# The two halves of a split weight chunk queued three blocks apart

## The chip, the cores and the metric

The kernel runs on one core of a Trainium2 chip. The metric is the time of one execution on the device in microseconds; lower is better. The time of before is the median of three runs.

## What is computed

The reference is a model of two parts on 512 tokens of width 1024, all in float32. The first part has a SwiGLU feed-forward, a mixer (sparse attention with 8 heads beside an S5 state-space branch), a second SwiGLU and a gated projection. The second part has two layers, each with an RG-LRU branch and an mLSTM branch, and a last RMS norm:

```python
h = x
h = h + 0.5 * swiglu(rmsnorm(h, norm_ffn1), w1, w3, w2)
z = rmsnorm(h, norm_mix) @ w_in
h = h + concat([nsa_attention(...), s5_mixer(...)]) @ w_out
h = h + 0.5 * swiglu(rmsnorm(h, norm_ffn2), ...)
h = h + sigmoid(rmsnorm(h, norm_ple) @ w_ple_gate) * (p @ w_ple)
x = rmsnorm(h, norm_final)
for l in range(2):
    u = (rms_norm(x, g) * (1 + scale) + shift) @ w_in[l]
    rg_x, rg_z, ml_x, ml_o, ml_z = split(u)
    y_rg = rglru(conv(rg_x), ...) * silu(rg_z)
    y_ml = mlstm_branch(conv(ml_x), ml_o, ...) * silu(ml_z)
    x = x + gate * (concat([y_rg, y_ml]) @ w_out[l])
return rms_norm(x, final_g)
```

Almost all of the work is products of the activations with weights that are read once.

## The kernel before

The 512 tokens lie along the free dimension, so that every product is a 128x128 block of weights against a 128x512 tile of activations, summed in PSUM. To keep float32 accuracy each operand is split in a high and a low part, and every block takes three matmuls (`mm3`, lines 121 to 127): high weight by high activation (L125), high weight by low activation (L126), low weight by high activation (L127).

The weights come as a stream of 304 chunks of eight blocks, packed on the host in the order in which the program asks for blocks (class `Stream`, lines 56 to 118). A chunk passes three steps. SyncE loads it (`wstage`, three buffers); ScalarE copies it, rounded, into the high part (`whi`, L96, four buffers); VectorE subtracts the high part from the loaded chunk and so gives the low part (`wlo`, L98, four buffers). TensorE then uses the two parts, eight blocks one after the other. Chunks 0 and 1 are split in halves, and GpSimd makes the second low half of chunk 1.

All of this is laid out by one program in one order, and each engine carries out its own instructions in the order in which the program put them into its queue. So what counts is where in the program an instruction is put. `get` (L109) is called once for each block, ahead of the block's matmuls, and it also puts the later chunks' steps into the queues: with the call for block 4 of chunk c, ScalarE's high part and VectorE's low part of chunk c + 2 and SyncE's load of chunk c + 4 (L114). While `hold` is set, at the end of a stage, only what is needed is put, and `release` (L71) makes up for it.

Between the calls of `get` the program puts the other steps: in the SwiGLU stages (L263) the gates on VectorE and ScalarE, and in the two layers a list written out by hand (`LAYER`, L1384), whose entries are short: `P10` is the product with column block 10 of the input weights, `U10` the use of its result, `rg1`, `rq1`, `rs2` the gates, the square root and the scan of the RG-LRU (L1839, L1863, L1868), `hn1`, `f1`, `F1` steps of the mLSTM head (L1743 to L1789), `rz2` its gate by silu. The output product of a layer follows the list; its result is added to the residual at L1938.

The names of tiles: `wstage`, `whi`, `wlo` as above; `xnh`, `xnl` the parts of the normalized activations; `pahead`, `pbhead`, `pagates`, `paout` and the like PSUM tiles of the two alternating banks, named by the stage; `rth`, `ra`, `rt`, `ry` of the RG-LRU; `n`, `dn`, `hr` of the mLSTM head's norm; `ymh`, `yml`, `yrh`, `yrl` high and low parts of the output product's right side; `t` of the SwiGLU gate; `s5yg`, `s5gw`, `cA`, `cAh` of the mixer.

Of the kernel before, what the change touches and what calls it, by code (L numbers as in the profile page):

```python
# [21 lines left out]
F32 = mybir.dt.float32  # L22
F32R = mybir.dt.float32r
I32 = mybir.dt.int32
BF = mybir.dt.bfloat16
AF = mybir.ActivationFunctionType
# [9 lines left out]
CH = 8  # L36
# [14 lines left out]
def room(pool, name):  # L51
    if GAPS[name]:
        pool.tile([128, GAPS[name] // 4], F32, name="gap", bufs=1)


class Stream:
# [2 lines left out]

    AHEAD = 2  # L60
    SPLIT = 2

    def __init__(self, k, dram, nchunks):
        self.k, self.dram, self.n = k, dram, nchunks
        self.order = []
        self.stage, self.hi, self.lo = {}, {}, {}
        self.loaded = self.split_done = 0
        self.pos = 0
        self.hold = False

    def release(self):  # L71

        self.hold = False
        self.split(self.pos // CH + 1 + self.SPLIT)

    def load(self, upto):
        k = self.k
        while self.loaded < min(upto, self.n):
# [3 lines left out]
            self.stage[c] = t  # L82
            self.loaded += 1

    def split(self, upto):
        k = self.k
        while self.split_done < min(upto, self.n):
            c = self.split_done
            self.load(c + 1)
            st = self.stage.pop(c)  # L90
            hi = k.whi.tile([128, CH * 128], F32R, name="whi")
            lo = k.wlo.tile([128, CH * 128], F32R, name="wlo")
            n = 2 if c < 2 else 1
            for i in range(n):
                s = slice(i * CH * 128 // n, (i + 1) * CH * 128 // n)
                k.nc.scalar.activation(hi[:, s], st[:, s], AF.Copy)  # L96
                eng = k.nc.gpsimd if c * i == 1 else k.nc.vector
                eng.tensor_sub(lo[:, s], st[:, s], hi[:, s].bitcast(F32))  # L98
            self.hi[c], self.lo[c] = hi, lo
            self.split_done += 1  # L100
            self.load(c + 1 + self.AHEAD)

    def align(self, n):
# [5 lines left out]
    def get(self, *blocks):  # L109

        n = len(blocks)
        c, r = divmod(self.pos, CH)
        assert r + n <= CH
        self.split(c + 1 + (0 if self.hold else self.SPLIT if r >= CH // 2 else self.SPLIT - 1))  # L114
        self.order += list(blocks)
        self.pos += n
        s = slice(r * 128, (r + n) * 128)
        return self.hi[c][:, s], self.lo[c][:, s]
# [1842 lines left out]
def body(tc, ins, out, dbg):  # L1961
    nc = tc.nc
    with ExitStack() as ctx:
# [6 lines left out]
        room(k.wst, "base")  # L1970
        k.whi = pool("whi", Stream.SPLIT + 2)
        k.wlo = pool("wlo", Stream.SPLIT + 2)
        k.work = pool("work", 2)
# [251 lines left out]
```

## Time and profile before

| | before |
|---|---|
| median of three runs | 1997.06 us |
| lowest and highest | 1995.61 and 1997.36 us |
| the profiled execution | 1996.86 us |
| its span | 1995.1 us |
| mean granted TensorE clock | 0.982 |
| TensorE busy | 1931.2 us |
| VectorE busy | 1311.4 us |
| ScalarE busy | 821.4 us |

The span runs from the first to the last instruction; the execution's own time is 1.8 us longer. The granted clock is a share of the full 2.4 GHz; where it was not 1 it was 0.5, that is 1.2 GHz. A timeline row gives the start of an instruction, its length and, in brackets, how long its engine had idled ahead of it and what ended that. The ends of matmuls are modelled, so that for TensorE the starts are what is read.

### The profile page before, as it was taken

To read this page: it belongs to the slowest core of one execution; us is meant where nothing else is said; L and a number is where in the kernel's file an instruction comes from. 1 tells how busy PE (TensorE), PEld (TensorE's weight loads), DVE (VectorE), ACT (ScalarE), POOL (GpSimd) and SP (SyncE) were. 2 spreads that over 40 slices of the span, in tenths; PEclk is the share of its full clock that TensorE was granted. 3 is DMA by queue.
4 is the path that set the end of the run, shared out by engine and by line. 5 is a ranking of instruction groups with operands and counts; after the bars stand their busy time and mean duration, and the time that the engine had idled before them with its cause. 6 is when DMAs were issued, how large, how long until landed. Compare 5 with 4: busy or idle time off the path is not lost. (4 is left out here: it accounts for less than half of the span.)

```text
span 1995.1 us, 24709 instructions
## 1 busy us (share of the span) xinstructions
PE 1931.2 (97%) x9320; PEld 1581.3 (79%) x9320; DVE 1311.4 (66%) x2157; ACT 821.4 (41%) x1233; POOL 164.4 (8%) x225
## 2 busy tenths in 40 slices
PE   8999999998999999999999799999999899999997
PEld 6888888887867888888878687888888677887886
DVE  7766576678655575665666675887763666877843
ACT  5323232436555432232244445555432354555521
POOL 1000000111233100000001100101000100101001
PEclk9999999998899999999999899999999899999999
DMA  5335445465301365455433143222242243222241
GB/s 184 103 116 154 158 139 159 143 194 171 103 1 33 117 218 180 158 197 190 162 104 92 55 147 118 74 75 86 88 153 87 64 156 109 70 89 86 74 155 56
DMA packets 101400, 240.10 MB, mean 120 GB/s; under 512 B 24472, under 2 KB 37528, under 8 KB 101280
## 3 DMA queue, kind: packets, MB, share of 16 engines
q1 hardware_dynamic: 100592, 237.82, 37.6%
q8 instruction: 73, 1.20, 0.2%
q10 hardware_dynamic: 688, 0.70, 0.1%
q14 instruction: 47, 0.39, 0.1%
HBM read 216.19 MB, written 21.10 MB: 119 GB/s over the span
## 5 line engine op out<-in xcount | busy, mean ns | idle before, releaser
L98 DVE TENSOR_TENSOR wlo<-wstage,whi 128x1024 fp32r<-128x1024 f32 (+1 forms) x305 | 377.3, 1245 | 147.6 <-ACT whi L96 143.8
L96 ACT ACTIVATE whi<-wstage 128x1024 fp32r<-128x1024 f32 (+1 forms) x306 | 314.0, 1045 | 139.9 <-PE pasecond L126 43.1
L276 ACT ACTIVATE t<-t 128x512 f32<-128x512 f32 x44 | 27.9, 634 | 158.5 <-DVE t L275 158.5
L127 PE MATMUL pahead<-xnh,wlo 128*128 128x512 f32 x208 | 81.3, 391 | 3.4 <-DVE wlo L98 3.4
L125 PE MATMUL pahead<-xnh,whi 128*128 128x512 f32 x208 | 83.3, 400 | 0.0
L153 POOL TENSOR_TENSOR nacc<-nacc,nsq 128x512 f32<-128x512 f32 x20 | 26.8, 1343 | 680.9 <-ACT nsq L149 680.9
L126 PE MATMUL pahead<-xnl,whi 128*128 128x512 f32 x208 | 81.1, 390 | 0.0
L125 PE MATMUL pbfirst<-xnh,whi 128*128 128x512 f32 x176 | 70.4, 400 | 7.6 <-ACT whi L96 6.5
L125 PE MATMUL pbhead<-xnh,whi 128*128 128x512 f32 x192 | 76.9, 400 | 0.0
L1509 DVE SCALAR_TENSOR_TENSOR conv<-cpad,vec,conv 128x512 f32<-128x512 f32 x96 | 72.2, 752 | 5.6
L127 PE MATMUL pbhead<-xnh,wlo 128*128 128x512 f32 x192 | 75.5, 393 | 0.0
L126 PE MATMUL pbhead<-xnl,whi 128*128 128x512 f32 x192 | 75.3, 392 | 0.0
L126 PE MATMUL pbfirst<-xnl,whi 128*128 128x512 f32 x176 | 69.5, 395 | 0.3 <-DVE xnl L222 0.3
L127 PE MATMUL pbfirst<-xnh,wlo 128*128 128x512 f32 x176 | 69.2, 393 | 0.0
L125 PE MATMUL pbsecond<-xnh,whi 128*128 128x512 f32 x176 | 68.9, 392 | 0.0
L125 PE MATMUL pafirst<-xnh,whi 128*128 128x512 f32 x176 | 68.7, 390 | 0.0
L127 PE MATMUL pafirst<-xnh,wlo 128*128 128x512 f32 x176 | 68.6, 390 | 0.0
L127 PE MATMUL pbsecond<-xnh,wlo 128*128 128x512 f32 x176 | 68.5, 389 | 0.0
L126 PE MATMUL pbsecond<-xnl,whi 128*128 128x512 f32 x176 | 68.5, 389 | 0.0
L126 PE MATMUL pafirst<-xnl,whi 128*128 128x512 f32 x176 | 68.5, 389 | 0.0
L127 PE MATMUL pasecond<-xnh,wlo 128*128 128x512 f32 x176 | 68.5, 389 | 0.0
L125 PE MATMUL pasecond<-xnh,whi 128*128 128x512 f32 x176 | 68.5, 389 | 0.0
(762 smaller groups left out, 5229.9 us busy)
## 6 DMA issues: line engine op xcount, KB each, us to landing
wstage<-in_wpack_dram SPq DMA_DIRECT2D x304, 512.0 KB, 3.7
adaw<-in_wada_dram SPq DMA_DIRECT2D x48, 512.0 KB, 4.5
scr_v<-vv SPq DMA_DIRECT2D x16, 256.0 KB, 2.2
vr<-scr_v SPq DMA_DIRECT2D x16, 256.0 KB, 4.4
xr<-scr_x SPq DMA_DIRECT2D x16, 256.0 KB, 5.8
h<-in_xT_dram SPq DMA_DIRECT2D x8, 256.0 KB, 5.8
s5vw<-scr_wq SPq DMA_DIRECT2D x64, 32.0 KB, 2.0
s5vb<-in_s5bq_dram SPq DMA_DIRECT2D x8, 256.0 KB, 2.7
```

The lines of the kernel that those rows point to most:

```text
L96: k.nc.scalar.activation(hi[:, s], st[:, s], AF.Copy)
L98: eng.tensor_sub(lo[:, s], st[:, s], hi[:, s].bitcast(F32))
L125: mm(ps, w[0], x[0], start=start, stop=False)
L126: mm(ps, w[0], x[1], start=False, stop=False)
L127: mm(ps, w[1], x[0], start=False, stop=stop)
L153: k.nc.gpsimd.tensor_add(self.acc[1], self.acc[1], sq)
L276: nc.scalar.activation(t1, t1, AF.Silu)
L1509: v.scalar_tensor_tensor(c, xp[:, 1 + j:1 + j + T], w(j), c, op0=OP.mult, op1=OP.add)
```

## The change

The step that put both parts of a chunk into the queues is taken apart. The high part of chunk c + 2 is now put into ScalarE's queue with the call for block 3 of chunk c, one block earlier than before. The low part is put into VectorE's queue, and the load of chunk c + 4 into SyncE's, with the call for block 6, two blocks later. The two parts, which were put together, are three blocks apart. `hold` and `release` work as before, and the first two chunks too.

```diff
@@ -60,4 +60,5 @@
     AHEAD = 2
     SPLIT = 2
+    HI, LO = 3, 6
 
     def __init__(self, k, dram, nchunks):
@@ -65,5 +66,5 @@
         self.order = []
         self.stage, self.hi, self.lo = {}, {}, {}
-        self.loaded = self.split_done = 0
+        self.loaded = self.high_done = self.low_done = 0
         self.pos = 0
         self.hold = False
@@ -83,20 +84,37 @@
             self.loaded += 1
 
-    def split(self, upto):
+    def pieces(self, c):
+        n = 2 if c < 2 else 1
+        return [slice(i * CH * 128 // n, (i + 1) * CH * 128 // n) for i in range(n)]
+
+    def high(self, upto):
+
         k = self.k
-        while self.split_done < min(upto, self.n):
-            c = self.split_done
+        while self.high_done < min(upto, self.n):
+            c = self.high_done
             self.load(c + 1)
-            st = self.stage.pop(c)
-            hi = k.whi.tile([128, CH * 128], F32R, name="whi")
-            lo = k.wlo.tile([128, CH * 128], F32R, name="wlo")
-            n = 2 if c < 2 else 1
-            for i in range(n):
-                s = slice(i * CH * 128 // n, (i + 1) * CH * 128 // n)
-                k.nc.scalar.activation(hi[:, s], st[:, s], AF.Copy)
-                eng = k.nc.gpsimd if c * i == 1 else k.nc.vector
-                eng.tensor_sub(lo[:, s], st[:, s], hi[:, s].bitcast(F32))
-            self.hi[c], self.lo[c] = hi, lo
-            self.split_done += 1
+            self.hi[c] = k.whi.tile([128, CH * 128], F32R, name="whi")
+            for s in self.pieces(c):
+                k.nc.scalar.activation(self.hi[c][:, s], self.stage[c][:, s], AF.Copy)
+                if c < 2:
+                    self.low_piece(c, s)
+            self.high_done += 1
+
+    def low_piece(self, c, s):
+        k = self.k
+        if c not in self.lo:
+            self.lo[c] = k.wlo.tile([128, CH * 128], F32R, name="wlo")
+        eng = k.nc.gpsimd if c == 1 and s.start else k.nc.vector
+        eng.tensor_sub(self.lo[c][:, s], self.stage[c][:, s], self.hi[c][:, s].bitcast(F32))
+
+    def split(self, upto):
+
+        self.high(upto)
+        while self.low_done < min(upto, self.n):
+            c = self.low_done
+            if c > 1:
+                self.low_piece(c, self.pieces(c)[0])
+            del self.stage[c]
+            self.low_done += 1
             self.load(c + 1 + self.AHEAD)
 
@@ -112,5 +130,7 @@
         c, r = divmod(self.pos, CH)
         assert r + n <= CH
-        self.split(c + 1 + (0 if self.hold else self.SPLIT if r >= CH // 2 else self.SPLIT - 1))
+        if not self.hold:
+            self.high(c + self.SPLIT + (r >= self.HI))
+        self.split(c + 1 + (0 if self.hold else self.SPLIT - 1 + (r >= self.LO)))
         self.order += list(blocks)
         self.pos += n
```

In the changed file the lines behind the class stand 20 lower, and the subtraction is L108. Two places show what moves on VectorE.

The first is in layer 0, between the gates of the RG-LRU (`rg1`) and product `P10`. Before, the low part of chunk 204 stood ahead of the steps `rq1`, `hn1` and `rs2`; `rth`, `ra` and `rt` are tiles of the RG-LRU, `n` is the mLSTM head's:

```order
L1805 TENSOR_TENSOR yml<-n_10426,ymh 128x512
L98 TENSOR_TENSOR wlo<-wstage,whi 128x1024
L1854 TENSOR_TENSOR rth<-rth,conv 128x512
L1855 TENSOR_SCALAR ra<-ra 128x512
L1857 SCALAR_TENSOR_TENSOR rt<-rth,ra 128x512
L1858 SCALAR_TENSOR_TENSOR ra<-rt,ra 128x512
L1854 TENSOR_TENSOR rth<-rth,conv 128x512
L1855 TENSOR_SCALAR ra<-ra 128x512
L1857 SCALAR_TENSOR_TENSOR rt<-rth,ra 128x512
L1858 SCALAR_TENSOR_TENSOR ra<-rt,ra 128x512
L1760 SCALAR_TENSOR_TENSOR n_10790<-sig,pahead_10779 128x512
L1760 SCALAR_TENSOR_TENSOR n_10805<-sig,pbhead_10794 128x512
```

Now the same rows go by, and the low part of chunk 204 stands behind the last row of the scan (`ry`); the wlo behind `rz` is that of chunk 205:

```order
L1875 TENSOR_SCALAR ra<-ra 128x512
L1877 SCALAR_TENSOR_TENSOR rt<-rth,ra 128x512
L1878 SCALAR_TENSOR_TENSOR ra<-rt,ra 128x512
L1780 SCALAR_TENSOR_TENSOR n_10786<-sig,pahead_10775 128x512
L1780 SCALAR_TENSOR_TENSOR n_10801<-sig,pbhead_10790 128x512
L1890 SCALAR_TENSOR_TENSOR rth<-rth 128x512
L1891 TENSOR_TENSOR rth<-rth,ra 128x512
L1892 TENSOR_SCALAR ra<-ra 128x512
L1894 SCALAR_TENSOR_TENSOR ry<-ra,rth 128x512
L108 TENSOR_TENSOR wlo<-wstage,whi 128x1024
L1539 SCALAR_TENSOR_TENSOR rz<-rz,pahead_10811 128x512
L108 TENSOR_TENSOR wlo<-wstage,whi 128x1024
```

The first low part of the rows of before moved past 14 rows, to the place where the next low part had stood. Layer 1 has the same.

The second is at the start of the output product of layer 0 (`yrl`, `yml` are low parts of its right side). Before, the first low part here is that of chunk 224 and the last that of chunk 225:

```order
L1882 TENSOR_TENSOR ry<-ry,rz 128x512
L1805 TENSOR_TENSOR yrl<-ry,yrh 128x512
L98 TENSOR_TENSOR wlo<-wstage,whi 128x1024
L1795 TENSOR_TENSOR n_11736<-n_11736,pc 128x512
L1795 TENSOR_TENSOR n_11751<-n_11751,pc 128x512
L1882 TENSOR_TENSOR ry<-ry,rz 128x512
L1519 SCALAR_TENSOR_TENSOR zs<-zs,pahead_11881 128x512
L1813 SCALAR_TENSOR_TENSOR n_11736<-n_11736,hg_5926,zs 128x512
L1805 TENSOR_TENSOR yrl<-ry,yrh 128x512
L1805 TENSOR_TENSOR yml<-n_11736,ymh 128x512
L98 TENSOR_TENSOR wlo<-wstage,whi 128x1024
```

Now the first is that of chunk 223 and the last that of chunk 224:

```order
L1902 TENSOR_TENSOR ry<-ry,rz 128x512
L108 TENSOR_TENSOR wlo<-wstage,whi 128x1024
L1825 TENSOR_TENSOR yrl<-ry,yrh 128x512
L1815 TENSOR_TENSOR n_11732<-n_11732,pc 128x512
L1815 TENSOR_TENSOR n_11747<-n_11747,pc 128x512
L1902 TENSOR_TENSOR ry<-ry,rz 128x512
L1539 SCALAR_TENSOR_TENSOR zs<-zs,pahead_11877 128x512
L1833 SCALAR_TENSOR_TENSOR n_11732<-n_11732,hg_5922,zs 128x512
L1825 TENSOR_TENSOR yrl<-ry,yrh 128x512
L1825 TENSOR_TENSOR yml<-n_11732,ymh 128x512
L108 TENSOR_TENSOR wlo<-wstage,whi 128x1024
```

The low part of chunk 224 moved past seven rows, and that of chunk 223 came down to a place just ahead of the first `yrl`.

## Rows read from the trace of the kernel before

**Rows 1.** The page, part 1: busy time, share of the span, instructions.

```profile
PE 1931.2 (97%) x9320; PEld 1581.3 (79%) x9320; DVE 1311.4 (66%) x2157; ACT 821.4 (41%) x1233; POOL 164.4 (8%) x225
```

**Rows 2.** The page, part 5: the low parts: busy, mean ns, idle before.

```profile
L98 DVE TENSOR_TENSOR wlo<-wstage,whi 128x1024 fp32r<-128x1024 f32 (+1 forms) x305 | 377.3, 1245 | 147.6 <-ACT whi L96 143.8
```

**Rows 3.** TensorE's waits: line waited for, us in all, times, longest.

```profile
PE pm L195 <- DVE ncol L213: 5.8, 3, 2.5
...
PE pahead L127 <- DVE wlo L98: 3.4, 2, 1.7
...
PE pc L1793 <- DVE hr L1786: 1.7, 2, 0.9
```

**Rows 4.** Timeline of VectorE, layer 0: start, length, instruction, idle before it.

```profile
1322.07 1.23 DVE L98 TENSOR_TENSOR wlo<-wstage,whi 128x1024 fp32r<-128x1024 f32 x1 [2.83 <-ACT whi L96]
...
1325.27 0.43 DVE L1855 TENSOR_SCALAR ra<-ra 128x512 f32<-128x512 f32 x1 [1.37 <-ACT ra L1849]
...
1333.95 1.23 DVE L1874 TENSOR_TENSOR_SCAN ry<-ra,rth 128x512 f32<-128x512 f32 x1
1335.09 1.20 DVE L98 TENSOR_TENSOR wlo<-wstage,whi 128x1024 fp32r<-128x1024 f32 x1
```

**Rows 5.** Timeline of TensorE there.

```profile
1328.57 0.39 PE L127 MATMUL pbhead<-xnh,wlo 128*128 128x512 f32 x1
...
1329.93 0.39 PE L127 MATMUL pbhead<-xnh,wlo 128*128 128x512 f32 x1
```

**Rows 6.** Timeline of VectorE, the same place of layer 1.

```profile
1762.69 1.20 DVE L98 TENSOR_TENSOR wlo<-wstage,whi 128x1024 fp32r<-128x1024 f32 x1
```

**Rows 7.** Timeline of TensorE there.

```profile
1756.57 0.39 PE L127 MATMUL pbhead<-xnh,wlo 128*128 128x512 f32 x1
```

**Rows 8.** Timeline of VectorE, around the output product of layer 0.

```profile
1448.61 1.22 DVE L1874 TENSOR_TENSOR_SCAN ry<-ra,rth 128x512 f32<-128x512 f32 x1
...
1470.39 0.69 DVE L1805 TENSOR_TENSOR yml<-n,ymh 128x512 fp32r<-128x512 f32 x1
```

**Rows 9.** Timeline of TensorE there.

```profile
1448.69 0.39 PE L127 MATMUL pbhead<-xnh,wlo 128*128 128x512 f32 x1
...
1460.62 0.65 PE L1793 MATMUL pc<-ident,hr 128*128 128x128 f32 x4 [0.86 <-DVE hr L1786]
...
1468.41 0.39 PE L127 MATMUL paout<-yrh,wlo 128*128 128x512 f32 x1
```

**Rows 10.** Timeline of VectorE, the convolutions of layer 0.

```profile
1172.83 0.69 DVE L1546 TENSOR_TENSOR xcl<-xcs,xch 128x512 fp32r<-128x512 f32 x1
```

**Rows 11.** Timeline of TensorE there.

```profile
1174.23 0.39 PE L127 MATMUL pagates<-xnh,wlo 128*128 128x512 f32 x1
```

**Rows 12.** Timeline of VectorE at the first gate.

```profile
35.06 1.23 DVE L98 TENSOR_TENSOR wlo<-wstage,whi 128x1024 fp32r<-128x1024 f32 x1
```

**Rows 13.** Timeline of TensorE at the first gate and in the mixer.

```profile
36.95 0.50 PE L125 MATMUL pbfirst<-xnh,whi 128*128 128x512 f32 x1 [0.84 <-DVE t L275]
...
485.66 0.50 PE L125 MATMUL pamix<-xnh,whi 128*128 128x512 f32 x1 [1.47 <-ACT whi L96]
```

**Rows 14.** The page, part 6: loads, KB each, us to landing.

```profile
wstage<-in_wpack_dram SPq DMA_DIRECT2D x304, 512.0 KB, 3.7
```

**Rows 15.** Timeline of TensorE at two waits of before.

```profile
463.97 0.76 PE L125 MATMUL pbmix<-xnh,whi 128*128 128x512 f32 x1 [4.83 <-DVE ropeo L612]
...
1393.19 0.50 PE L127 MATMUL pahead<-xnh,wlo 128*128 128x512 f32 x1 [1.72 <-DVE wlo L98]
```

**Rows 16.** Windows of TensorE: us, busy (instructions), granted clock, DMA share, GB/s.

```profile
462.00:466.00 4.00, 2.03 (x4) 0.50 0.60 164
466.00:470.00 4.00, 4.00 (x14) 0.68 0.41 118
1394.00:1398.00 4.00, 4.00 (x27) 1.00 0.71 225
```

More of the change, by code (lines that the diff above doesn't have):

```diff
@@ L83, in load @@
             self.loaded += 1
-    def split(self, upto):
-        k = self.k
-        while self.split_done < min(upto, self.n):
-            c = self.split_done
-            self.load(c + 1)
-            st = self.stage.pop(c)
-            hi = k.whi.tile([128, CH * 128], F32R, name="whi")
-            lo = k.wlo.tile([128, CH * 128], F32R, name="wlo")
-            n = 2 if c < 2 else 1
-            for i in range(n):
-                s = slice(i * CH * 128 // n, (i + 1) * CH * 128 // n)
-                k.nc.scalar.activation(hi[:, s], st[:, s], AF.Copy)
-                eng = k.nc.gpsimd if c * i == 1 else k.nc.vector
-                eng.tensor_sub(lo[:, s], st[:, s], hi[:, s].bitcast(F32))
-            self.hi[c], self.lo[c] = hi, lo
-            self.split_done += 1
+    def pieces(self, c):
[5 more added lines that the diff above has]
+            c = self.high_done
+            self.load(c + 1)
+            self.hi[c] = k.whi.tile([128, CH * 128], F32R, name="whi")
[5 more added lines that the diff above has]
+    def low_piece(self, c, s):
+        k = self.k
+        if c not in self.lo:
+            self.lo[c] = k.wlo.tile([128, CH * 128], F32R, name="wlo")
+        eng = k.nc.gpsimd if c == 1 and s.start else k.nc.vector
+        eng.tensor_sub(self.lo[c][:, s], self.stage[c][:, s], self.hi[c][:, s].bitcast(F32))
+    def split(self, upto):
+        self.high(upto)
[5 more added lines that the diff above has]
+            self.low_done += 1
             self.load(c + 1 + self.AHEAD)
```

## The prediction

> **What bounds the kernel now.** Read the page first. TensorE is busy for 97% of the span, VectorE for 66% [rows 1]: the time is the sum of TensorE's matmuls and of its waits, so an edit that changes no matmul can act only through the waits. The list of what TensorE waits for comes second: in the whole span it waits for the low part of a weight (wlo) only a few times, 3.4 us in the largest group [rows 3]. Yet VectorE itself idles 147.6 us ahead of its 305 wlo, of which 143.8 until ScalarE has made the high part [rows 2]. So wlo is made as soon as it can be, and waits in a buffer for TensorE. How long, the timelines tell: each place was read for three times, the wlo, the rows of VectorE that now stand ahead of it, and the first matmul of line 127 that reads it. That is the whole method below.
>
> **The change, part by part.** No instruction is added or removed. The orders of TensorE and GpSimd stay; 20 high parts on ScalarE move up, by one to six rows but for one; some 150 of VectorE's 303 low parts move down, and with them some 22 weight loads in SyncE's queue stand a few places later. A queue runs in order, so a wlo that stands n rows later can start only when the last of these rows has ended, and ends about 1.22 us later (1.20 and 1.23 in [rows 4]). If that is later than its first matmul, TensorE stands still for the difference, since every later matmul is queued behind.
>
> *The long places, two.* In layer 0 the wlo of chunk 204 ran at 1322.07 [rows 4]; its first use is at 1329.93 [rows 5], a slack of 6.6 us. It now stands behind the 14 rows that follow it (square root, head and scan of the RG-LRU and mLSTM steps; the order listing shows both ends). Two of them wait for ScalarE, the first 1.37 us for ra [rows 4], so taking the wlo out from ahead of them does not start them earlier. The last ends at 1333.95 + 1.23 = 1335.18, and the wlo takes the slot that the next one had, 1335.09 to 1336.29 [rows 4]. Late by 1336.29 - 1329.93 = 6.4 us. The reason: block 4 of chunk 202, where the low part was put before, lies ahead of these steps in the program, block 6 behind them, ten blocks ahead of the use; two blocks are 1.36 us [rows 5], so ten are 6.8. Layer 1 has the same place: the slot ends at 1762.69 + 1.20 = 1763.89 [rows 6], the use was at 1756.57 [rows 7]: 7.3 us. **Together 13.7.** A lower bound takes off 1.37 and as much again at each, if ScalarE should after all be earlier: 8.2; upwards only the clock adds, below.
>
> *The head of the output product, twice.* The wlo of chunk 221 goes behind six rows, the last of which ends at 1448.61 + 1.22 = 1449.83 [rows 8]; its use was at 1448.69 [rows 9]. With its own 1.22 it is late by up to 2.4 us; by 1.2 if the six rows close up over the gap that it leaves; I take 1.95, as a second wlo also moves in among them. TensorE's wait of 0.86 for hr behind it [rows 9] then goes, as VectorE has that time to finish. The wlo of chunk 224 goes behind seven rows to 1470.39 + 0.69 = 1471.08 [rows 8] with its use at 1468.41 [rows 9], by then some 1.1 later: 1.2 to 2.8, taken as 1.2, since the rows ahead of it move up. Net 1.95 - 0.86 + 1.2 = 2.3, and the same in layer 1: **4.6**, bounds 2 and 8.
>
> *Ten single places.* There the last passed row ends within about one wlo of the use. Chunk 182 is the pattern: 1172.83 + 0.69 + 1.22 = 1174.74 [rows 10] against 1174.23 [rows 11], late by 0.5. The ten come to 0.15 to 1.45 each, **5.0** in all; the bounds are 0 (rows close up) and 12 (one whole wlo each).
>
> *Gains, two.* At the first gate a wlo of 1.23 us [rows 12] stands ahead of t (line 275), for which TensorE waited 0.84 [rows 13]; that wlo moves behind t: **-0.84**. In the mixer VectorE's wlo goes behind the rows that ScalarE's cAh waits for, and ScalarE's next high part, for which TensorE waits 1.47 us [rows 13], comes earlier: between 0 and -1.47, taken as **-1.1**.
>
> *The rest costs nothing.* In the two SwiGLU stages, the gated projection and the rest of the layers the passed rows end early enough that a wlo fits in ahead of its use; TensorE's own products cover the move, and a cover that is gone would show as one more single place, at most 1.2 us. Later loads are covered too: a load takes 3.7 us [rows 14] and is put three chunks ahead, 24 blocks of 0.68 us, over 16 us.
>
> *The clock.* Behind a wait of 4.83 us the granted clock was 0.50, that is 1.2 GHz, and came back to 2.4 GHz within the next window [rows 15, 16]: at half from 463.97 to 466, and for (1 - 0.68)/0.5 = 0.64 of the four us behind that, 4.6 us, of which half is lost: 2.3 us. Behind the wait of 1.72 us it stayed at 1.00 [rows 15, 16]. The two long waits, 6.4 and 7.3, are nearer to the first: **+4.6**, bounds 0 and 2 x 3.
>
> The Trainium skill (TensorE: Matmul & The Clock Gate, What's actually happening) says the array's clock has two rates, and goes back to the lower when the array has been idle; the rows at 463.97 agree. By it the two long waits cost this term too, and the sum is the one below; without it the sum would be 4.6 us less.
>
> **Sum:** 13.7 + 4.6 + 5.0 - 0.8 - 1.1 + 4.6 = 26.0 us on the profiled execution's 1996.86, which is 0.2 under the median of the runs: **2023 us**, 1.3% slower. A difference of 0.2%, 4 us, is about what a measurement of this kernel can tell from none.
>
> **Rivals.**
> - *Only the long waits count.* Behind them VectorE is so far ahead that later rows close up, the places of the output product and the single ones are absorbed, and the clock holds: 13.7 - 1.9 = 11.8, **2009 us**. For it: VectorE has a third of its time free [rows 1]. Against: the output product is some 100 us behind the long wait, and its rows wait for TensorE's products, so they shift with it. Chance 0.2.
> - *TensorE's work decides, nothing changes.* With 97% busy [rows 1] and 66% on VectorE, a lo could be late without being missed, if the slacks read here are those of the modelled ends: **1997 us**. Against: the slack at 1329.93 is between two starts, and the wait of 1.72 for a wlo [rows 15] shows that TensorE stops for a late one at once. Chance 0.06. The Trainium skill (Perfetto Trace Analysis, Identifying the Most-Contended Engine) would have one improve the engine of the highest occupancy first; by that, work moved on another engine leaves 1997, which the waits of this trace speak against.
> - *Faster: the idle time ahead of the low parts gets used.* VectorE's queue no longer stands at a wlo until the high part is there (2.83 us ahead of chunk 204's, [rows 4]). If the 14 rows start 2.83 + 1.22 earlier and the wait of 1.37 goes as well, they end 5.4 us sooner, the wlo is late by 1.0 and 1.9 only, and wherever TensorE waits for VectorE a wlo of up to 1.22 us is gone from the chain: three times ncol, twice hr [rows 3], 3 x 1.22 + 1.7 + 0.8 + 1.1 = 7.3, net -4.4: **1992 us**. It decides for itself if the 14 rows end before 1328.7. Against: ra waits for ScalarE, which is not earlier, and the ncol chains mostly stand where no wlo does. Chance 0.05.
> - *A cascade.* A late wlo also frees its staging buffer late; the load, the high part and the next low part follow. One further wait behind each long one, of a load (3.7 us [rows 14]) and a wlo (1.22), some 5 us each: 26 + 10, **2033 us**. Against: three chunks of matmuls lie between. Chance 0.07.
>
> **How the numbers follow.** Forecast 0.62, its own range 2011 to 2034: below, all lower ends with the clock (8.2 + 2 + 0 - 0.8 + 4.6 = 14); above, 13.7 + 8 + 12 - 0.8 + 4.6 = 37.5 at once is unlikely, and about the half of what the upper ends add is let in. The rivals have 0.2, 0.06, 0.05 and 0.07. The range of 8 in 10 takes in the first rival and the cascade: 2008 to 2034. Faster by over 0.2% is the third rival, 0.05; within it the second, 0.06; slower all else, 0.89.
>
> **What would show it.** Right: two new waits of TensorE for wlo at line 127's matmuls of the head products, 6 to 7 us each, in both layers, and the clock at half behind them; waits of 1 to 2 us for wlo at the output product; wlo's own idle time on VectorE down from 147.6; no wait for t at the first gate. Wrong: if the 14 rows end before the use, if waits for wlo sum to under 8 us, or if the added time sits in waits for whi or for loads, my account has failed.

## The result and the profile after

The change made the kernel slower: 2020.16 us (median of four runs, 2017.81 to 2027.04) against 1997.21 for the kernel before. The recorded ratio is 1.0121 with a 95% interval of 1.0095 to 1.0146; the two medians alone give 1.0115. The forecast was 2023, range 2008 to 2034. The profiled execution of after took 2020.39 us, its span is 2018.6, 23.5 more than before.

TensorE's busy time grew by 5.8 us (1931.2 before, [rows 1]); the other 17.7 of the 23.5 are in its waits. Page part 1 of after, and from part 5 the row of the low parts (busy, mean ns, idle before):

```profile
PE 1937.0 (96%) x9320; PEld 1581.3 (78%) x9320; DVE 1314.9 (65%) x2157; ACT 820.9 (41%) x1233; POOL 171.3 (8%) x225
...
L108 DVE TENSOR_TENSOR wlo<-wstage,whi 128x1024 fp32r<-128x1024 f32 (+1 forms) x305 | 384.4, 1268 | 68.2 <-ACT whi L98 68.1
```

VectorE now idles 68.2 us ahead of its low parts, against 147.6 [rows 2]: when a low part's turn comes, its high part has more often been made. That is the part of the change that works, and it is on an engine whose idle time there cost nothing: with half of it gone the kernel is slower. What TensorE waits for in after (us in all, times, longest):

```profile
PE pbhead L147 <- DVE wlo L108: 16.0, 6, 6.2
...
PE pahead L147 <- DVE wlo L108: 3.4, 2, 1.7
...
PE pagates L147 <- DVE wlo L108: 3.1, 6, 1.2
...
PE paout L147 <- DVE wlo L108: 2.4, 2, 1.2
...
PE pamix L145 <- ACT whi L98: 0.9, 1, 0.9
```

The first group did not exist before; the second is that of [rows 3], unchanged; the third was one wait of 0.5 before; the fourth is new; the last was 1.47 [rows 13]. Now the first of the long places, VectorE's timeline of after (start, length, instruction, idle before it):

```profile
1330.59 1.23 DVE L1894 TENSOR_TENSOR_SCAN ry<-ra,rth 128x512 f32<-128x512 f32 x1
1331.73 1.20 DVE L108 TENSOR_TENSOR wlo<-wstage,whi 128x1024 fp32r<-128x1024 f32 x1
1332.85 0.68 DVE L1539 SCALAR_TENSOR_TENSOR rz<-rz,pahead 128x512 f32<-128x512 f32 x1
1333.44 1.22 DVE L108 TENSOR_TENSOR wlo<-wstage,whi 128x1024 fp32r<-128x1024 f32 x1
1340.12 0.16 DVE L1796 SCALAR_TENSOR_TENSOR dn<-pc,em 128x4 f32<-128x4 f32 x1 [5.46 <-PE pc L1794]
```

The low part of chunk 204 stands behind the scan (`ry`), where [rows 4] has that of chunk 205, and ends at 1332.93. On TensorE's timeline of after, the matmul that reads it starts 0.06 us later; its twin in layer 1 starts 0.05 us behind its low part. The two shorter rows are those at the head of the output product:

```profile
1332.99 0.80 PE L147 MATMUL pbhead<-xnh,wlo 128*128 128x512 f32 x1 [6.20 <-DVE wlo L108]
...
1457.31 0.50 PE L147 MATMUL pbhead<-xnh,wlo 128*128 128x512 f32 x1 [1.47 <-DVE wlo L108]
...
1477.44 0.50 PE L147 MATMUL paout<-yrh,wlo 128*128 128x512 f32 x1 [1.18 <-DVE wlo L108]
...
1774.59 0.80 PE L147 MATMUL pbhead<-xnh,wlo 128*128 128x512 f32 x1 [6.19 <-DVE wlo L108]
```

In [rows 5, 7, 9] these four matmuls had no wait. Behind the long ones the clock was at half, that is 1.2 GHz, until about 1336.2 and 1779.9 (estimates from the shares of the windows of after; us, busy, granted clock, DMA share, GB/s):

```profile
1330.00:1334.00 4.00, 1.01 (x2) 0.50 0.08 9
1334.00:1338.00 4.00, 4.00 (x14) 0.73 0.72 228
1772.00:1776.00 4.00, 1.41 (x3) 0.63 0.13 19
1776.00:1780.00 4.00, 4.00 (x11) 0.51 0.74 235
```

### The profile page after: what moved, and what is told of

The parts are those of the page before. It is cut to its first block, busy times and chain, and to the rows that moved or that the text cites. A ratio compares the mean times of both kernels' runs of the same rounds, so it can differ in the third digit from the quotient of the medians.

```text
span 2018.6 us, 24650 instructions
## 1 busy us (share of the span) xinstructions
PE 1937.0 (96%) x9320; PEld 1581.3 (78%) x9320; DVE 1314.9 (65%) x2157; ACT 820.9 (41%) x1233; POOL 171.3 (8%) x225
## 5 line engine op out<-in xcount | busy, mean ns | idle before, releaser
L108 DVE TENSOR_TENSOR wlo<-wstage,whi 128x1024 fp32r<-128x1024 f32 (+1 forms) x305 | 384.4, 1268 | 68.2 <-ACT whi L98 68.1
L146 PE MATMUL pasecond<-xnl,whi 128*128 128x512 f32 x176 | 68.5, 389 | 0.0
```

Of the source, the lines that this page charges most:

```text
L108: eng.tensor_sub(self.lo[c][:, s], self.stage[c][:, s], self.hi[c][:, s].bitcast(F32))
L146: mm(ps, w[0], x[1], start=False, stop=False)
```

## The experiments

The theory under test, called A in the expectations, is that of the prediction: a low part costs TensorE the time by which the last row that stands ahead of it on VectorE ends too late; neither the block by itself nor the high part matters. Its rivals: B, the earlier high part disturbs ScalarE's queue; C, the loss grows with the distance in blocks. Every ratio is the recorded one, against runs of the kernel before on the same chip.

**One half of the change at a time.** First the high part is put back to its block, then the low part:

```diff
-    HI, LO = 3, 6
+    HI, LO = 4, 6
```

> The high part put back to block 4, the low part left at block 6. Theory A (the place of the low part in VectorE's queue costs, the high part's block costs nothing): 2020 us, within 2 of the changed kernel, with the two waits of 6.2 us for wlo in the head products still there. Rival B (what costs is that the high part goes into ScalarE's queue ahead of the steps that VectorE's rows wait for): back to 1998 to 2005. Rival C (the loss grows with the distance of the low part in blocks): 2020 as A.

Measured: 2021.32 us, ratio 1.0121 (1.0104 to 1.0138), as slow as the change. The group of waits at the head products is 15.9 us in 6, the longest 6.2.

```diff
-    HI, LO = 3, 6
+    HI, LO = 3, 4
```

> The low part put back to block 4, the high part left at block 3. Theory A: 1997 us, within 2 of the kernel before, with no wait for wlo at the head product's place in rg1 to P10. Rival B: 2010 or more. Rival C: 1997 as A.

Measured: 1996.14 us, ratio 0.9994 (0.9984 to 1.0003): no difference from before, and no wait at the head products but the old ones of 1.7. B falls; the whole loss comes with the low part. The load of chunk c + 4 moves with it in SyncE's queue, but it is not what is waited for: in after the low part of chunk 204 starts behind the scan with no idle time ahead of it, so its high part and its load were there, and scan_behind, below, leaves the loads where the change has them.

**One block less, one block more.**

```diff
-    HI, LO = 3, 6
+    HI, LO = 3, 5
```

> High part at block 3, low part at block 5, one block ahead of the change. By the order of the program the low part of chunk 204 then stands ahead of the 14 rows again, as before. Theory A: the two long waits and the clock behind them are gone, what is left are some of the short ones and the gains of the front: 1995 to 2002 us. Rival C (loss by distance in blocks, two blocks cost 23 us): one block costs about half, 2008 to 2012.

Measured: 1994.99 us, ratio 0.9991 (0.9979 to 1.0002). One block later than before costs nothing, two cost 23 us: C falls on this side. The traces say why: in this run only seven low parts come to stand behind other rows of VectorE than before, in the change 143. Blocks 2 to 5 of chunk 202 belong to `rg1`, whose gates come behind its last block, and only block 6 is called behind the 14 rows. Nor does the number of rows decide: in after the low parts of chunks 131 and 160 stand 24 rows later and that of chunk 194 stands 17 rows later, and TensorE waits for none of the three.

```diff
-    HI, LO = 3, 6
+    HI, LO = 3, 7
```

> The low part one block later still, block 7. By the order of the program VectorE's queue in the two layers stays as in the change: no step lies between block 6 and block 7 there; ahead of the layers some low parts move past a few rows. Theory A: 2020 to 2023 us, the long waits 6.2 us as in the change. Rival C (distance in blocks, some 11 us a block): 2030 or more.

Measured: 2026.47 us, ratio 1.0141 (1.0125 to 1.0157), 3.5 us above what A expected. The total lies between A's range and C's 2030, so the waits have to decide. In the layers they are those of the change, as A says: 6.20 twice, and 1.47 and 1.19 at the output product. New are two waits in the mixer, ahead of the layers, in the list of this run:

```profile
PE pbhead L147 <- DVE wlo L108: 16.0, 6, 6.2
PE pc L865 <- DVE wlo L108: 9.7, 2, 6.8
...
PE pbmix L147 <- DVE wlo L108: 6.5, 2, 6.2
```

There the low parts had come to stand behind the S5 scan and the rotary rows; the timeline of VectorE in this run, and then that of TensorE:

```profile
464.52 0.68 DVE L632 SCALAR_TENSOR_TENSOR ropeo<-pbmix,ropet 128x512 f32<-128x512 f32 x1
465.12 1.22 DVE L108 TENSOR_TENSOR wlo<-wstage,whi 128x1024 fp32r<-128x1024 f32 x1
...
473.16 0.98 DVE L636 TENSOR_TENSOR q<-q,ropeb 128x512 f32<-128x512 f32 x1
474.06 3.19 DVE L108 TENSOR_TENSOR wlo<-wstage,whi 128x1024 fp32r<-128x1024 f32 x2
```

```profile
466.39 0.57 PE L865 MATMUL pc<-wlo,cAh 128*124 128x256 f32 x1 [6.79 <-DVE wlo L108]
...
475.32 0.79 PE L147 MATMUL pbmix<-xnh,wlo 128*128 128x512 f32 x1 [6.23 <-DVE wlo L108]
```

It is the same mechanism at another place; the "few rows" that these low parts pass ahead of the layers had been taken for cheap without reading their times. The two groups are 14.2 us longer than in after (9.7 and 6.5 against 1.7 and 0.3), the span only 8.3, mainly because after's wait of 6.5 us for ropeo at the same place is gone here: one wait took the place of another.

**The two long places, undone and alone.**

```diff
-        self.split(c + 1 + (0 if self.hold else self.SPLIT - 1 + (r >= self.LO)))
+        low = 4 if c in (202, 266) else self.LO
+        self.split(c + 1 + (0 if self.hold else self.SPLIT - 1 + (r >= low)))
```

> The change, but in chunks 202 and 266 the low part (of chunks 204 and 268) is put at block 4 as before. Theory A: 12.4 us of waits and about 3.4 to 4.5 us of half clock behind them go: 2003 to 2005 us, the other waits for wlo stay as they are in the changed kernel. A rival by which the two waits only bring forward what would be lost later anyway (VectorE behind its work): over 2012.

Measured: 2007.73 us, ratio 1.0057 (1.0040 to 1.0075): more than half of the loss is gone, but the time is 3 us above what was expected. The reason is in its waits for wlo at the head products:

```profile
PE pbhead L148 <- DVE wlo L108: 6.2, 4, 1.6
```

Of 16.0 us 9.8 are gone, not 12.4: chunk 206 (270 in layer 1), behind the long place, now makes TensorE wait 1.63 us where it was 0.33 with the long wait ahead of it. A long wait covers part of the next. The reverse:

```diff
-        self.split(c + 1 + (0 if self.hold else self.SPLIT - 1 + (r >= self.LO)))
+        low = self.LO if c in (202, 266) else 4
+        self.split(c + 1 + (0 if self.hold else self.SPLIT - 1 + (r >= low)))
```

> The low part at block 4 everywhere as before, but in chunks 202 and 266 at block 6: only the two long places of the change. Theory A: 2 x 6.2 us of wait and 1.6 to 2.4 us of half clock behind each, on 1996 to 1997: 2012 to 2014 us, with no other new wait for wlo over 1 us. Rival (VectorE makes up for two waits where nothing else is late): under 2005.

Measured: 2012.79 us, ratio 1.0074 (1.0058 to 1.0091), with just the two long waits in that group:

```profile
PE pbhead L148 <- DVE wlo L108: 12.4, 2, 6.2
```

So two of the 143 moved low parts make two thirds of the loss: 15.2 us here against 23.0. With the 10.3 that two_undone is above before that is 25.5, and the 2.6 of cover at chunks 206 and 270 are the difference.

**The rows ahead, not the block.** The low part stays where the change puts it, and the scan is written behind the product (a piece of the one long line of the list):

```diff
...
-rg1 rq1 hn1 rs2 P10 U10 P11
+rg1 rq1 hn1 P10 rs2 U10 P11
...
```

> The change, with one entry of the layers' list moved: the scan rs2 stands behind product P10 instead of ahead of it, so that in each layer the four rows of the scan (4.0 us from their start to their end) come behind the low part of chunk 204 or 268. Block and distance of the low part stay as in the change. Theory A (the rows that stand ahead of the low part make it late): each long wait falls from 6.2 to 2.2 us, and the clock holds behind it: 2008 to 2012 us. Rival C (distance in blocks): the waits stay, 2020.

Measured: 2008.64 us, ratio 1.0055 (1.0036 to 1.0073). Both long waits are 2.22 us, 3.98 less, which is the length of the four rows taken from ahead of the low part (1327.73 to 1331.73 in after, 4.00). Block and load are those of the change; this is the most direct test of the mechanism. One part of the expectation failed: the clock held behind one of the two waits only, see the last section.

**What is worth keeping.** Three runs: the low part's move only ahead of the layers, with the high part at block 3 everywhere; the parts at block 4 as before but in chunks 211 and 275, where both parts (those of chunks 213 and 277) are put at block 1; and the two together. The last of the three diffs is against the one before it.

```diff
-        self.split(c + 1 + (0 if self.hold else self.SPLIT - 1 + (r >= self.LO)))
+        low = self.LO if c < 166 else 4
+        self.split(c + 1 + (0 if self.hold else self.SPLIT - 1 + (r >= low)))
```

> High part at block 3; low part at block 6 up to chunk 165, at block 4 from there: the change only ahead of the layers. Theory A: the losses are all in the layers, so what is left are the gains ahead of them (first gate 0.8, gated projection 1.9, mixer and others near 0): 1994 to 1996 us. A rival by which the gains ahead of the layers are no more than chance of one execution: 1996 to 1999.

Measured: 1995.29 us, ratio 0.9988 (0.9979 to 0.9997), some 2 us below before.

```diff
+        high, low = (4, 4)
+        if c in (211, 275):
+            high = low = 1
         if not self.hold:
-            self.high(c + self.SPLIT + (r >= self.HI))
-        self.split(c + 1 + (0 if self.hold else self.SPLIT - 1 + (r >= self.LO)))
+            self.high(c + self.SPLIT + (r >= high))
+        self.split(c + 1 + (0 if self.hold else self.SPLIT - 1 + (r >= low)))
```

> Both parts at block 4 as before, but in chunks 211 and 275 at block 1: only the two waits of 1.72 us are meant to go. Theory A: 1997.4 - 3.4 = 1994 us. If the rows that the earlier parts push back make another wait: 1996 to 1998.

Measured: 1992.92 us, ratio 0.9980 (0.9970 to 0.9989), 1 us below what was expected.

```diff
-        high, low = (4, 4)
+        high, low = (self.HI, self.LO) if c < 166 else (3, 4)
```

> A version meant to beat both: low part at block 6 only up to chunk 165 (the stages ahead of the layers, where the change gained), at block 4 in the layers, and in chunks 211 and 275 both parts at block 1, so that the low parts of chunks 213 and 277 come ahead of the gate and scan rows that made TensorE wait 1.72 us for each of them before. Theory A: 3.4 us of waits go in the layers and 1 to 3 us ahead of them: 1991 to 1994 us. If the front's gains belong to single executions: 1993 to 1995.

Measured: 1990.47 us, ratio 0.9965 (0.9951 to 0.9978): 7.1 us below before, 29.7 below the change, and 0.5 below the range expected. The matmul of [rows 15] that waited 1.72 us runs without a wait, on TensorE's timeline of this run:

```profile
1389.74 0.39 PE L150 MATMUL pahead<-xnh,wlo 128*128 128x512 f32 x1
```

**Before once more.** A second profiled execution of the kernel before, without an edit, gives what belongs to single executions.

> The kernel before as it is, for a second profiled execution: which waits of TensorE and which stretches at half clock come again. Theory A needs none of its terms from here; the waits behind steps of VectorE should come again within 0.3 us, while those behind GpSimd's nacc and the half-clock stretches without a wait ahead of them may differ.

Measured: 2001.78 us in its one execution. The waits for wlo at the head products (3.4 in 2) came again. So did the wait for nacc in the gated projection, which I had expected to vary: 1.75 us, 1.78 in the first profile. Two waits for VectorE in the mixer did not come again within the 0.3 us expected: 6.50 us for ropeo, 4.83 in the first profile, and 2.87 for a wlo (line 845), 0.69 in the first. So the 6.5 for ropeo in after need not be of the change. The stretches at half clock differed too; more on that below.

## Why the prediction was right

The path was the forecast one, and its terms held, measured as growth of the delay of the same matmul between the traces of before and after (its start in after less its start in before, a few matmuls ahead of the place against a few behind it; at the long waits up to the first matmul behind the wait):

- *The two long places*: 13.7 forecast; the waits are 6.20 and 6.19, the delay grew by 12.7. Layer 0 was right within 0.2. Layer 1 was put at 7.3 from the slot of [rows 6]; there ScalarE's last `rth` had ended 1.62 us behind the first matmul of P10, against 0.61 in layer 0, and in after it ends 0.60 behind it in both. So a chain that I took to be fixed by ScalarE came one microsecond earlier. Two long waits alone (two_alone) and shortened by the scan's own length (scan_behind) show the cause.
- *The head of the output product*: 2.3 forecast per layer; measured 2.2 in both. The three parts are 1.8, -1.1 and 1.5 in layer 0 (forecast 1.95, -0.86, 1.2).
- *Ten single places*: 5.0 forecast. Eight new small waits for wlo show, at 0.59 to 0.93 of delay each, 5.3 together; chunk 182, the one that is worked out in the prediction, cost 0.60 for 0.5. Two more places grew that were no part of the sum: an old wait for wlo (1151.84 in before's time) by 0.75, and a wait for ScalarE in the attention (636.09) by 0.8.
- *The gains*: the wait for t at the first gate went (1.1 for 0.84), the wait for the high part in the mixer fell by 0.56 (1.1 forecast). One gain of 1.72 was not seen ahead: TensorE's wait for nacc in the gated projection, 1.78 before and 0.06 in after.
- *The clock*: 4.6 forecast; behind the two long waits the delay grew by 1.6 and 2.6 while the clock was at half, 4.2. The Trainium skill's rule (TensorE: Matmul & The Clock Gate, What's actually happening), that the array goes back to the lower rate when it has been idle, agrees with both.

In sum 26.0 forecast, 23.7 in the traces (the last matmul's delay) and 23.0 between the medians. The forecast terms alone measure 25.0. That the total is so near besides is in part luck: what was not forecast is +1.6 at the two places more, +3.2 in two stretches at half clock (last section), -1.7 at nacc, and some -4 left over in small waits and in half-clock stretches elsewhere that the two executions do not share.

Of the rivals, "only the long waits count" would have been 2009: two_undone says that 10 us of loss are left without them. "TensorE's work decides" falls with all of it: all that moved was work of other engines than the busiest one, and it cost 23 us. The Trainium skill (Perfetto Trace Analysis, Identifying the Most-Contended Engine) says to optimize the engine of the highest occupancy first; that tells where to look for a gain, and it is no forecast that a move on another engine costs nothing. "Faster" asked that the 14 rows start earlier without the low part ahead of them; they did not, because VectorE then waited that much longer for ScalarE's ra, 2.50 us against 1.37 [rows 4], as this row of after shows:

```profile
1321.95 0.43 DVE L1875 TENSOR_SCALAR ra<-ra 128x512 f32<-128x512 f32 x1 [2.50 <-ACT ra L1869]
```

The scan then ended at 1331.82, 1335.12 in before's time at this place, against 1335.18 before. The cascade did not come: no wait for a late load was found, and two_undone shows the reverse, a long wait covering the next.

The one unforeseen gain: VectorE's and ScalarE's chain for the gated projection ran some 1.8 us behind TensorE in the kernel before. The wait stands in both profiles of before and in that of low213_alone, which moves neither part there; it is gone in the other nine runs and in after, in lo_back (high part alone) as in hi_back (low part alone). So either move removes it; which of the moved instructions does, was not tried. It is probably most of what front_late keeps, with the wait for t.

## What to carry to other kernels

An engine's idle time ahead of an instruction is no cost by itself: the change took VectorE's wait for high parts from 147.6 us to 68.2, and the kernel lost 23. Nor does it measure the slack: in two_alone that idle time is 133.1 us and the loss 15.2, in two_undone 72.1 and the loss 10.3. When a step is put later in a queue, take each place, not the mean: the end of the last row now ahead of it plus its own length, against the start of its first reader. Of 143 low parts that moved, most cost nothing and two made two thirds of the loss, where the rows between the old and the new place end behind the first use; the remedy is to put it, or these rows, elsewhere at such places alone: two_undone and scan_behind each took back half of the loss.

## What was not expected of the hardware

The clock fell without a long wait too, in one execution and not in the next. In before, behind the wait of 1.72 us at 1393.19, the granted clock was 1.00 [rows 15, 16]. The second execution of the same program had waits of 1.71 and 1.68 us at these places; the windows behind each:

```profile
1394.00:1398.00 4.00, 4.00 (x27) 1.00 0.73 199
1398.00:1402.00 4.00, 4.00 (x19) 1.00 0.53 195
1820.00:1824.00 4.00, 2.32 (x16) 1.00 0.27 58
1824.00:1828.00 4.00, 4.00 (x14) 0.51 0.82 286
1828.00:1832.00 4.00, 4.00 (x13) 0.64 0.13 51
```

Behind the first it ran at 2.4 GHz, behind the second at 1.2 GHz for some 6.8 of the eight us from 1824 (an estimate from the two shares). In scan_behind two waits of the same 2.22 us, at 1328.59 and 1761.37, stood the same way apart:

```profile
1328.00:1332.00 4.00, 3.41 (x15) 1.00 0.43 132
1332.00:1336.00 4.00, 4.00 (x27) 1.00 0.20 28
...
1760.00:1764.00 4.00, 2.63 (x6) 0.68 0.38 108
1764.00:1768.00 4.00, 4.00 (x24) 0.89 0.08 28
```

And in after it was at 0.63 and 0.66 in these two windows; the first begins 1.5 us behind the end of an old wait of 1.73 us, the second has no wait of TensorE in it or in the 8 us ahead of it:

```profile
1400.00:1404.00 4.00, 4.00 (x19) 0.63 0.86 298
1724.00:1728.00 4.00, 4.00 (x20) 0.66 0.00 0
```

Together these two stretches cost after 3.2 us, of the 23.7. So the waits of 6.2 us had the clock at half behind them in each of the runs that has them (after, hi_back, lo_seven, two_alone), and behind waits of about 2 us it differed from one execution, and one place, to the next. What decides is left open. It is likely part of why single executions of one kernel here stand up to 9 us apart (before: 1993.79 to 2002.84; of the four of after, the one of 2027.04 had a mean granted clock of 0.973, the others 0.979 to 0.980), and it is why a term of 1 us is better read from the waits than from the total.
